# A causal depthwise convolution: five of eight channel tiles as block Toeplitz products

## The chip, the cores and the metric

The kernel runs on one core of one Trainium2 chip. The metric is the device time of one execution in microseconds (us). The core has TensorE (PE, with its weight loads shown apart as PEld), VectorE (DVE), ScalarE (ACT), GpSimd (POOL) and SyncE (SP); each works through its own list of instructions in order. SP issues nearly all DMA transfers.

## The reference

A decoder trunk of two layers on x of 512 positions by 1024 features, in float32:

```
layer 0: mix = [S5 state space | stick-breaking attention](x W_in) W_out
layer 1: h = x W_pw1 + b;  h = h[:, :1024] * sigmoid(h[:, 1024:])
         h[t, c] = sum_k w_dw[k, c] * h[t - 30 + k, c] + b_dw[c]      (31 taps, causal)
         mix = silu(LN(h)) W_pw2 + b
each layer:  x = LN(alpha x + mix);  x = LN(alpha x + relu(x W1 + b1)^2 W2 + b2)
```

The hidden width of the feed-forward layers is 4096. The change bears on layer 1's depthwise convolution.

## The kernel before, in words

Features lie on the partitions: x is eight tiles of 128 features by 512 positions. Every matrix product is made in three products of float32r operands, each operand split into a rounded high part and a low part (`whi`, `wlo`, `xbh`, `xbl`): high by high, high by low, low by high. The class `Weights` loads a weight chunk with SP (`raw`, two buffers), rounds it on ACT (`whi`, L90) and subtracts on DVE (`wlo`, L91), a few units ahead of the product that uses them, into a ring of 3 + 5 slots. Tiles in the trace bear the names of the code: `f` and `acf` are the two products of a feed-forward block, `hh` and `hl` its hidden activations' parts, `pl` the first pointwise product (pw1) of the convolution's tiles 0 and 1, `pv` and `pg` value and gate of the others, `tld` the second pointwise product (pw2), `fl` the next feed-forward layer's first.

The program's stages by the trace: the mix layer to 246 us, its output product and LN a to 306, feed-forward layer 0 to 598 (four blocks of eight hidden tiles), its tail and LN b to 651, pl to 673, the convolution to 812, the second half of LN c and pw2 (tld) to 871, then LN d, feed-forward layer 1 and the transposed output.

The convolution before: a tile's gated input (`hp`, with 30 columns of zeros ahead) is convolved by PE and DVE together. PE takes the first taps of a tile, each as three products with a diagonal 128x128 matrix of the tap's weights, which ACT has made just before (`dh`, `dl`, L136); how many is a table, PE_TAPS. DVE takes the others as multiply-and-add over the whole tile into two accumulators (`cy`, `cz`, L339). The last two tiles are worked in halves of 256 columns, so that the first half of the norm (LN c: `mpc`, `vpc`, `sc`, `sqc`) and of pw2 can begin before their second halves are convolved:

```python
PE_TAPS = ((5, 8, 10, 10, 9, 11, 17, 16), (10, 10, 10, 10, 10, 10, 13, 14))
SPLIT_TILES = 2
```

The order of the work comes from the order in which the code is written and from a scheduler, which places instructions of each engine by their priority and by modelled times; in the mix layer a list of words (`ORDER`) sets it. Thirteen small loads of bias and norm vectors (`rows`) and two transposes of them (`pvp`, L606) stand ahead of that list's steps.

Of the kernel before, what the change touches and what calls it, by code (L numbers as in the profile page):

```python
# [16 lines left out]
P = 128  # L17
# [18 lines left out]
PE_TAPS = ((5, 8, 10, 10, 9, 11, 17, 16), (10, 10, 10, 10, 10, 10, 13, 14))  # L36
DBUFS = 6
SPLIT_TILES = 2
GLU_FIRST = True
FFN_BLOCKS = ((8, 8, 8, 8), (8, 8, 6, 4, 6))  # L40
LEAD = 6
AHEAD = (5, 4)
# [7 lines left out]
ORDER = "q0 s0 y0 s1 y1 a0 q1 s2 y2 a1 s3 y3 q2 gelu a2 q3 glu a3".split()  # L50


class Weights:


    def __init__(self, tc, ahead):
        self.tc, self.nc, self.ahead = tc, tc.nc, ahead
        self.slots, self.units, self.raw, self.urgent, self.fence, self.hold = [], [], None, True, None, False
        self.done, self.got, self.chunk, self.ready = 0, 0, {}, {}
# [17 lines left out]
    def _prep(self, n):  # L77
        nc = self.nc
        while self.done < min(n, len(self.units)):
            key, src, nk, ncol, off, width = self.units[self.done]  # L80
            self.fetch(self.done)
            raw = self.chunk[key][:, :, off : off + ncol]
            pool, s = self.slots[self.done % len(self.slots)]
# [43 lines left out]
class Act:  # L127
# [5 lines left out]
    def __call__(self, out, in_, func, **kw):  # L133
# [10 lines left out]
        self.run.append(ins.name)  # L144


@with_exitstack
def kernel(ctx: ExitStack, tc: tile.TileContext, a: dict, out: bass.AP):
# [442 lines left out]


    rows = s5.tile([P, 2, P], F32, tag="sp", name="rows", bufs=6)
    G.memset(rows, 0.0)
    for n in vecs:
        src = a[n].rearrange("a (r f) -> (a r) f", f=P)
        r0, m = vrow[n], a[n].shape[0] * a[n].shape[1] // P
        done = 0
        while done < m:
            half, at = divmod(r0 + done, P)  # L600
            c = min(m - done, P - at)
            nc.sync.dma_start(rows[at : at + c, half, :], src[done : done + c])
            done += c
    pvp = zz("pvp")
    for i in range(2):
        PE.transpose(pvp[:, i * P : (i + 1) * P], rows[:, i, :], ident)  # L606
    V.tensor_copy(PV, pvp[:, :nrow])
# [132 lines left out]
    for o in ORDER:  # L740
        if o[0] == "q":
            hq[o[1]] = qkv(int(o[1]))
        elif o[0] == "a":
            attention(int(o[1]), *hq[o[1]])
        elif o[0] == "s":
            s5_states(int(o[1]))
        elif o[0] == "y":
            s5_outputs(int(o[1]))
        elif o[0] == "t":
            tables(int(o[1]))  # L750
        elif o == "gelu":
            gelu()
        else:
            glu()

    def accum(nps, xk, name, ncol, first=True, cols=((0, T),)):
# [3 lines left out]
        for c0, c1 in cols:  # L760
            for j in range(KT):
# [7 lines left out]
                else:  # L769
                    tt(x, x, ps[:, c0:c1], ALU.add)  # L770

# [25 lines left out]

    units = units_of("mo", w_out, 4, 4, range(0, D, 256), 512)
    for layer in range(2):
        if layer:  # L800
            for j in range(0, D, 128):
                units += units_of("pw1", a["conv_w_pw1"][0], 0, 8, [j], 256)
                units += units_of("pw1", a["conv_w_pw1"][0], 0, 8, [D + j], 256)
# [15 lines left out]
    class LN:  # L819


        def __init__(self, name):
            self.n, self.s = name, {}

        def add(self, j, ys, c0, c1):

            if j == 1:
                self.s[c0] = tmp(f"s{self.n}{c0}")[:, c0:c1]
            if j:
                (V if j == KT - 1 else G).tensor_tensor(self.s[c0], ys[0][:, c0:c1] if j == 1 else self.s[c0], ys[j][:, c0:c1], op=ALU.add)  # L830
# [53 lines left out]
    class Tail:  # L884
# [7 lines left out]
        def run(self, n):  # L892

            nj = KT // len(self.xk)
            for _ in range(n):
# [9 lines left out]
                self.ln.add(j, X, c0, c1)  # L905
# [39 lines left out]
    def ffn1(layer, bi, k0, nb, xs, fps, first=()):  # L945
        hs = []
        for i in range(nb):
# [12 lines left out]
            hs.append((hh, hl))  # L960
        return hs
# [7 lines left out]
    xs, first = tail_norm_lead(cat[4:8], "a", rb[0], ("ln1_g", 0), ("ln1_b", 0), LEAD, "fl0")  # L969
    k0 = 0  # L970
    for bi, nb in enumerate(FFN_BLOCKS[0]):
        hs = ffn1(0, bi, k0, nb, xs, nps, first if bi == 0 else ())
        if bi < len(FFN_BLOCKS[0]) - 1:
            accum(nps, hs, f"f0{bi}", 1024 // nb, bi == 0)
        k0 += nb
    wdw = hid.tile([P, KT, CONV], F32, tag="wdw", name="wdw")
    for f in range(2):
        wn = tmp(f"wn{f}")[:CONV]
        nc.sync.dma_start(wn, a["conv_w_dw"][0][:, f * T : (f + 1) * T])
        ps = stp(f"wd{f}")  # L980
        for i in range(4):
            PE.transpose(ps[:, i * 32 : i * 32 + CONV], wn[:, i * P : (i + 1) * P], ident[:CONV, :CONV])
        V.tensor_copy(wdw[:, 4 * f : 4 * f + 4, :], ps[:, :P].rearrange("p (i t) -> p i t", t=32)[:, :, :CONV])
    wdh = hid.tile([P, KT, CONV], F32R, tag="wdh", name="wdh")
    wdl = hid.tile([P, KT, CONV], F32, tag="wdl", name="wdl")
    V.tensor_copy(wdh, wdw)
    V.tensor_sub(wdl, wdw, wdh.bitcast(F32))

# [3 lines left out]
    acc = [None] * KT  # L992
    hps = [None] * KT
    cps = [None] * KT

    def glu_tile(j, c0=0, c1=T):
        if c0 == 0:
            if j < 2:
                ps[j] = first[2 * j : 2 * j + 2]
            else:  # L1000
                ws[j], ps[j] = (W.next(), W.next()), (nps(f"pv{j}"), nps(f"pg{j}"))
            hps[j] = hpage(f"hp{j}", F32, PAD + T), hpage(f"hph{j}", F32R, PAD + T), hpage(f"hpl{j}", F32R, PAD + T)
        vps, gps = ps[j]
        if j >= 2:
            gemm(vps, ws[j][0], slice(0, P), xs, c0, c1)
            gemm(gps, ws[j][1], slice(0, P), xs, c0, c1)
        sg = tmp(f"csg{j}{c0}")
        act(sg[:, c0:c1], gps[:, c0:c1], AF.Sigmoid, bias=pv("conv_b_pw1", 8 + j))
        hp, hh, hl = hps[j]
        p0 = PAD + c0 if c0 else 0  # L1010
        if c0 == 0:
            V.memset(hp[:, :PAD], 0.0)
        stt(hp[:, PAD + c0 : PAD + c1], vps[:, c0:c1], pv("conv_b_pw1", j), sg[:, c0:c1], ALU.add, ALU.mult)
        split(hh[:, p0 : PAD + c1], hl[:, p0 : PAD + c1], hp[:, p0 : PAD + c1])

    def taps_pe(j, c0=0, c1=T):
        _, hh, hl = hps[j]
        if c0 == 0:
            cps[j] = nps(f"cv{j}")
        n = PE_TAPS[c0 > 0][j]  # L1020
        for t in range(n):
            dh = hid.tile([P, P], F32R, tag="dh", name=f"dh{j}{t}", bufs=DBUFS)
            dl = hid.tile([P, P], F32R, tag="dl", name=f"dl{j}{t}", bufs=DBUFS)
            act(dh, ident, AF.Copy, scale=wdh.bitcast(F32)[:, j, t : t + 1])
            act(dl, ident, AF.Copy, scale=wdl[:, j, t : t + 1])
            for i, (u, v) in enumerate(((dh, hh), (dh, hl), (dl, hh))):
                PE.matmul(cps[j][:, c0:c1], u, v[:, t + c0 : t + c1], start=t == 0 and i == 0, stop=t == n - 1 and i == 2)  # L1027

    def taps_dve(j, c0=0, c1=T):

        hp = hps[j][0]
        if c0 == 0:
            acc[j] = page(f"cy{j}", F32), hpage(f"cz{j}", F32)
        y, z = (x[:, c0:c1] for x in acc[j])
        t = CONV - 1
        act(y, hp[:, t + c0 : t + c1], AF.Identity, bias=pv("conv_b_dw", j), scale=wdw[:, j, t : t + 1])
        t = CONV - 2
        opened = act(z, hp[:, t + c0 : t + c1], AF.Copy, scale=wdw[:, j, t : t + 1])
# [159 lines left out]
```

## Time and profile before

| what | value |
|---|---|
| median of 3 runs | 1244.07 us (1242.49 to 1245.63) |
| the profiled execution | 1245.87 us, its span 1244.2 us |
| TensorE clock granted, mean | 0.984 |
| PE busy | 1198.7 us, 96% of the span |
| DVE / ACT / POOL busy | 778.6 / 567.7 / 105.8 us |
| DMA moved | 105.93 MB, mean 85 GB/s |

In the profile, rows are groups of instructions or links of the chain that ended last; a row names start, duration, engine, tiles and line, or for groups the busy time, the mean duration of one in ns and the idle time ahead of them with its releaser.

### The profile page before, as it was taken

How to read it: one execution, taken by the hardware profiler on the slowest of the kernel's cores; microseconds unless marked ns; L12 is line 12 of the kernel's file. 1: busy time of each engine (PE TensorE's matmuls, PEld its weight loads, DVE VectorE, ACT ScalarE, POOL GpSimd, SP SyncE). 2: the span in 40 equal slices, each digit the busy share in tenths (PEclk: the TensorE clock that was granted, in tenths of full speed). 3: DMA queues.
4: the chain of work that ended last, by engine and by line, in shares of the span. 5: the costliest groups of instructions: out<-in, count | busy, mean ns of one | idle time of the engine just before them, and what ended most of it. 6: DMA issues, size and time to landing. Idle time of an engine off the chain costs nothing.

```text
span 1244.2 us, 16659 instructions
## 1 busy us (share of the span) xinstructions
PE 1198.7 (96%) x6559; PEld 1016.9 (82%) x6559; DVE 778.6 (63%) x1321; ACT 567.7 (46%) x1020; POOL 105.8 (9%) x145
## 2 busy tenths in 40 slices
PE   9899999999999999999999999689899999999997
PEld 7677776789988888888999889689898888888885
DVE  7897784568734434434388999999863443444446
ACT  6735665734523313314246666876472232323230
POOL 1001100122000000000130012113400000000000
PEclk9999998999999999999999999889899999999999
DMA  8510131050522333322232121003052232323211
GB/s 207 161 36 18 35 110 60 21 200 1 186 88 100 102 102 102 100 81 91 73 103 86 51 68 35 1 28 110 17 186 68 85 119 68 124 68 113 86 51 68
DMA packets 111663, 105.93 MB, mean 85 GB/s; under 512 B 9379, under 2 KB 99747, under 8 KB 111585
## 3 DMA queue, kind: packets, MB, share of 16 engines
q1 hardware_dynamic: 111424, 104.84, 26.9%
q8 instruction: 51, 0.84, 0.3%
q14 instruction: 28, 0.22, 0.1%
q10 hardware_dynamic: 160, 0.03, 0.0%
HBM read 100.66 MB, written 4.19 MB: 84 GB/s over the span
## 4 chain that ended last, share of the span: by engine, by line
PE 75%; DVE 15%; ACT 5%; DMA 2%; issue 2%; POOL 1%; SPq 0%; DVEq 0%; ACTq 0%; POOLq 0%
PE f L207 23%; PE g L1128 11%; PE acf L207 11%; PE fl L207 4%; PE h L1112 3%; PE tld L207 3%; DVE cz L339 3%; PE tlb L207 2%; PE cv L1027 2%; DVE wlo L91 2%; DVE cy L339 2%; PE pl L207 1%; PE pv L207 1%; PE pg L207 1%; DVE X L339 1%
## 5 line engine op out<-in xcount | busy, mean ns | idle before, releaser
L90 ACT CAST whi<-raw 128x1024 fp32r<-128x1024 f32 x176 | 183.9, 1049 | 400.1 <-PE f L207 111.9
L91 DVE TENSOR_TENSOR wlo<-raw,whi 128x1024 fp32r<-128x1024 f32 x176 | 219.5, 1251 | 221.0 <-ACT whi L90 220.7
L1128 PE MATMUL g<-whi,hh 128*128 128x512 f32 x208 | 81.5, 392 | 0.0
L1128 PE MATMUL g<-wlo,hh 128*128 128x512 f32 x208 | 81.5, 392 | 0.0
L1128 PE MATMUL g<-whi,hl 128*128 128x512 f32 x208 | 81.4, 391 | 0.0
L207 PE MATMUL f<-xdh,whi 128*128 128x512 f32 x208 | 80.9, 389 | 0.0
L207 PE MATMUL f<-xah,whi 128*128 128x512 f32 x208 | 80.9, 389 | 0.0
L207 PE MATMUL f<-xal,whi 128*128 128x512 f32 x208 | 80.9, 389 | 0.0
L207 PE MATMUL f<-xdh,wlo 128*128 128x512 f32 x208 | 80.9, 389 | 0.0
L207 PE MATMUL f<-xdl,whi 128*128 128x512 f32 x208 | 80.9, 389 | 0.0
L207 PE MATMUL f<-xah,wlo 128*128 128x512 f32 x208 | 80.9, 389 | 0.0
L207 PE MATMUL acf<-hl,whi 128*128 128x512 f32 x192 | 75.2, 392 | 0.0
L207 PE MATMUL acf<-hh,whi 128*128 128x512 f32 x192 | 74.9, 390 | 0.0
L207 PE MATMUL acf<-hh,wlo 128*128 128x512 f32 x192 | 74.7, 389 | 0.0
L197 ACT CAST hh<-fr 128x512 fp32r<-128x512 f32 x64 | 39.7, 621 | 71.4 <-DVE fr L335 71.4
L198 DVE TENSOR_TENSOR hl<-fr,hh 128x512 fp32r<-128x512 f32 x64 | 44.2, 691 | 37.3 <-ACT hh L197 37.2
L339 DVE SCALAR_TENSOR_TENSOR cy<-hp,wdw,cy 128x512 f32<-128x512 f32 (+1 forms) x91 | 60.8, 678 | 0.1
L339 DVE SCALAR_TENSOR_TENSOR cz<-hp,wdw,cz 128x512 f32<-128x512 f32 (+1 forms) x86 | 59.7, 698 | 0.0
L1027 PE MATMUL cv<-hph,dh 128*128 128x256 f32 (+1 forms) x113 | 40.0, 354 | 10.0 <-ACT hph L197 8.3
L335 DVE TENSOR_TENSOR fr<-fr 128x512 f32<-128x512 f32 x64 | 43.7, 685 | 5.4 <-ACT fr L136 5.4
L1128 PEld LDWEIGHTS g<-whi,hl 128*128 128x128 f32 x208 | 39.1, 188 | 8.6
L1128 PEld LDWEIGHTS g<-wlo,hh 128*128 128x128 f32 x208 | 39.1, 188 | 8.5
(684 smaller groups left out, 3172.3 us busy)
## 6 DMA issues: line engine op xcount, KB each, us to landing
raw<-in_ffn_w_dram SPq DMA_DIRECT2D x48, 1024.0 KB, 5.3
raw<-in_ffn_w_dram SPq DMA_DIRECT2D x32, 512.0 KB, 3.6
raw<-in_conv_w_pw_dram SPq DMA_DIRECT2D x12, 1024.0 KB, 5.4
raw<-in_mix_w_in_dram SPq DMA_DIRECT2D x16, 512.0 KB, 4.2
xin<-in_x_dram SPq DMA_DIRECT2D x8, 256.0 KB, 3.8
raw<-in_s_w_glu_dram SPq DMA_DIRECT2D x4, 512.0 KB
raw<-in_mix_w_out_dram SPq DMA_DIRECT2D x4, 512.0 KB
raw<-in_mix_w_out_dram SPq DMA_DIRECT2D x2, 1024.0 KB, 6.3
```

Source lines behind the costliest of these rows:

```text
L90: i0 = nc.scalar.copy(hi, raw).ins
L91: i1 = nc.vector.tensor_sub(lo, raw, hi.bitcast(F32)).ins
L197: i0 = S.copy(hi, src).ins
L198: i1 = V.tensor_sub(lo, src, hi.bitcast(F32)).ins
L207: ins = PE.matmul(ps[:, c0:c1], u[:, k, ksl], v[:, c0:c1], start=start and k == 0 and i == 0, stop=stop and k == n - 1 and i == 2).ins
L335: V.tensor_tensor(o, x, y, op=op)
L339: V.scalar_tensor_tensor(o, x, s, y, op0=op0, op1=op1)
L1027: PE.matmul(cps[j][:, c0:c1], u, v[:, t + c0 : t + c1], start=t == 0 and i == 0, stop=t == n - 1 and i == 2)
L1112: PE.matmul(ps, u, v, start=k == 0 and i == 0, stop=k == nk - 1 and i == 2)
L1128: PE.matmul(pss[b], u, v[:, kk, :], start=k + kk == 0 and i == 0, stop=k + kk == nb - 1 and i == 2)
```

## The change

1. Tiles 2 to 6 are convolved wholly on PE. A tile's input is laid out in four time phases: 32 channels by four phases make the 128 partitions, so that a product with a 128x128 matrix of Toeplitz blocks takes four taps at once for four phases of output. Nine shifts cover the 31 taps; with four groups of 32 channels and three products each, a tile takes 108 products of 128 columns.
2. The matrices are made on DVE in feed-forward layer 0 from block 1 on: 90 multiplications of 128x512 (`m`), each a broadcast of tap weights times a mask, one pair behind a hidden tile or an accumulation (`make`). SP writes each (256 KB) to DRAM (`made`). The tap weights come by way of DRAM too (`Wd`, `w4`: 16 small loads for each tile).
3. In the convolution POOL reads the matrices back with 50 transfers, two for a unit of eight matrices (512 KB each, high and low parts), through a second `Weights` (`M`) that has four slots of the ring; units of pw1 use the other four.
4. The input's phase layout is made by a round trip through DRAM (`Hd`, four loads `hr`); the output of tiles 6, 2 and 3 goes back the same way (`Od`, `cq`), that of tiles 4 and 5 by sixteen 32x128 operations, half on ACT and half on DVE.
5. Tiles 0, 1 and 7 are convolved wholly on DVE: 29 multiply-and-adds each. There are no halves any more. The work's order is a list of words (`CONV_ORDER`).
6. LN c takes a provisional centre from the first five finished tiles, subtracts it and adds up squares as tiles come; the rest of the mean follows with the last tile. Its sums are on DVE instead of POOL.
7. The `rows` loads and pvp's transposes move into the mix layer's list, behind `a0`.

```diff
-PE_TAPS = ((5, 8, 10, 10, 9, 11, 17, 16), (10, 10, 10, 10, 10, 10, 13, 14))
-DBUFS = 6
-SPLIT_TILES = 2
+ON_PE = (2, 3, 4, 5, 6)
+CONV_ORDER = "g0 g1 d0 g6 d0 d0 d1 g7 d0 s6 g2 d1 m6 o6 d1 x1 f6 d1 s2 g3 m2 o2 d7 x0 s3 d7 g4 m3 f2 o3 d7 d7 s4 g5 c0 m4 s5 f3 e4 m5 e5".split()
-ORDER = "q0 s0 y0 s1 y1 a0 q1 s2 y2 a1 s3 y3 q2 gelu a2 q3 glu a3".split()
+ORDER = "q0 s0 y0 s1 y1 a0 rows q1 s2 y2 a1 s3 y3 q2 gelu a2 q3 glu a3".split()
...
+            if key[0] == "made":
+                w = tuple(pool.tile([P, nk, ncol], F32R, tag=f"w{x}{s}", name=f"w{x}{self.done}", bufs=1) for x in ("hi", "lo"))
+                for x, d in zip(w, src):
+                    nc.gpsimd.dma_start(x.rearrange("p k n -> p (k n)")[:, : d.shape[1]], d)
...
+    bias4 = hid.tile([P, KT, 4], F32, tag="bias4", name="bias4")
+    for q in range(4):
+        nc.sync.dma_start(bias4[32 * q : 32 * q + 32], a["conv_b_dw"][0].rearrange("(j g c) -> c j g", g=4, c=32))
+
+    def matrices(i):
...
+        for p_ in range(4):
+            for g in range(4):
+                nc.sync.dma_start(wr[32 * p_ : 32 * p_ + 32, NU * g : NU * (g + 1)], Wd[32 * g : 32 * g + 32, i, p_ : p_ + NU])
+        V.tensor_copy(wh, wr)
+        V.tensor_sub(wl, wr, wh.bitcast(F32))
+        for u in range(0, 4 * NU, 16):
+            for x, src in enumerate((wh.bitcast(F32), wl)):
+                m = tmp(f"m{j}{x}{u}", F32R)
+                V.tensor_tensor(m.rearrange("p (u c) -> p u c", c=GROUP), src[:, u : u + 16].unsqueeze(2).broadcast_to([P, 16, GROUP]),
+                                mask.unsqueeze(1).broadcast_to([P, 16, GROUP]), op=ALU.mult)
+                nc.sync.dma_start(made[j][x][:, u * GROUP : (u + 16) * GROUP], m.bitcast(F32))
+            yield
...
-            accum(nps, hs, f"f0{bi}", 1024 // nb, bi == 0)
+            accum(nps, hs, f"f0{bi}", 1024 // nb, bi == 0, after=make if bi else None)
...
+    def toeplitz(j):
+
+        hh, hl = hps[j]
+        cp = nps(f"cv{j}")
+        for g in range(4):
+            o = cp[:, g * P : (g + 1) * P]
+            for e in range(SHIFTS):
+                n = SHIFTS * g + e
+                if n % 8 == 0:
+                    w = M.next()
+                mh, ml = (x[:, n % 8] for x in w)
+                for k, (u, v) in enumerate(((mh, hh), (mh, hl), (ml, hh))):
+                    PE.matmul(o, u, v[:, g, e : e + P], start=e == 0 and k == 0, stop=e == SHIFTS - 1 and k == 2)
...
+        elif o[0] == "m":
+            toeplitz(j)
+        elif o[0] == "c":
+            center()
...
-        for j in range(n, KT):
-            taps_dve(j, c0, c1)
...
+        r = conv_norm(c0, c1)
```

In `CONV_ORDER` g makes a tile's gated input, s splits its phases, m makes its products, o, f and e bring it back, d is a piece of eight taps on DVE, c the provisional centre, x prepares the residual.

Three places in the engines' lists. First DVE within feed-forward layer 0, where `fr` and `hl` make a hidden tile and `wlo` a weight's low half. Before:

```order
L335 TENSOR_TENSOR fr_3909<-fr_3909 128x512
L198 TENSOR_TENSOR hl_3913<-fr_3909,hh_3912 128x512
L91 TENSOR_TENSOR wlo_4030<-raw_4027,whi_4029 128x1024
L335 TENSOR_TENSOR fr_3945<-fr_3945 128x512
L198 TENSOR_TENSOR hl_3949<-fr_3945,hh_3948 128x512
```

and after:

```order
L1045 TENSOR_TENSOR m_4085<-w4h_3850,mask 128x512
L1045 TENSOR_TENSOR m_4088<-w_3849,mask 128x512
L351 TENSOR_TENSOR fr_4078<-fr_4078 128x512
L106 TENSOR_TENSOR wlo_4178<-raw_4134,whi_4177 128x1024
L214 TENSOR_TENSOR hl_4082<-fr_4078,hh_4081 128x512
L1045 TENSOR_TENSOR m_4127<-w4h_3850,mask 128x512
```

Two multiplications have come in with each hidden tile, and stand ahead of the next one's `fr`.

Second PE at the end of the convolution. Before, the last products of a first half, with the first mean product between them, and pw1 of other halves ahead:

```order
L207 MATMUL pg_6904<-xbh_5443,wlo_6565 128x256
L1027 MATMUL cv_6988<-hph_6731,dh_7457 128x256
L1027 MATMUL cv_6988<-hpl_6732,dh_7457 128x256
L1027 MATMUL cv_6988<-hph_6731,dl_7458 128x256
L838 MATMUL mpc_7366<-sc_6393,ones 128x256
L1027 MATMUL cv_6988<-hph_6731,dh_7464 128x256
```

and after:

```order
L1117 MATMUL cv_7585<-hl_7547,whi_7614 128x128
L1117 MATMUL cv_7585<-hh_7546,wlo_7615 128x128
L1204 MATMUL mpc_7729<-cy_7550,ones 128x256
L1204 MATMUL mpc_7729<-cy_7559,ones 128x256
L1205 MATMUL vpc_7730<-sqc_7398,ones 128x256
L1204 MATMUL mpc_7729<-cy_7702,ones 128x256
L1206 MATMUL vpc_7730<-sqc_7723,ones 128x256
```

All convolution products now stand ahead of the norm's, and nothing of the convolution stands between them any more; `cy_7702` is the last tile's output.

Third SP in the same stage, after the change (before, it has only raw weights there):

```order
L71 DMA raw_7865<-in_conv_w_pw_dram 128x8x256
L1093 DMA Hd_7150<-hp_7145 128x544
L1097 DMA hr_7152<-Hd_7150 32x4x136 x4
L1125 DMA Od_7294<-cr_7292 128x512
L1129 DMA cq_7296<-Od_7294 32x4x128 x4
L1093 DMA Hd_7387<-hp_7382 128x544
L1097 DMA hr_7389<-Hd_7387 32x4x136 x4
L71 DMA raw_7875<-in_conv_w_pw_dram 128x8x256
```

The round trips of tiles 4 and 5 stand with the output of tile 3 between two loads of pw2's weights.

More of the change, by code (lines that the diff above doesn't have):

```diff
@@ L960, in ffn1 @@
             hs.append((hh, hl))
+            if layer == 0 and bi:
+                make()
         return hs
@@ L970, with make @@
+    def make():
+        for _ in range(1):
+            next(making, None)
+    making = (None for i in range(NT) for _ in matrices(i))
     k0 = 0
     for bi, nb in enumerate(FFN_BLOCKS[0]):
+        if bi == 1:
+            taps()
         hs = ffn1(0, bi, k0, nb, xs, nps, first if bi == 0 else ())
         if bi < len(FFN_BLOCKS[0]) - 1:
-            accum(nps, hs, f"f0{bi}", 1024 // nb, bi == 0)
+            accum(nps, hs, f"f0{bi}", 1024 // nb, bi == 0, after=make if bi else None)
         k0 += nb
-    wdw = hid.tile([P, KT, CONV], F32, tag="wdw", name="wdw")
@@ L977 @@
[L977 to L985, printed above, removed]
@@ L1016, in taps_pe @@
[L1016 to L1027, printed above, removed]
```

332 lines of the change are left out of this document (233 added, 99 removed).

## The prediction

> **What bounds the kernel now.** I read the page's busy times first, then the busy times stage by stage, then the chain that ended last.
>
> ```profile
> span 1244.2 us, 16659 instructions
> PE 1198.7 (96%) x6559; PEld 1016.9 (82%) x6559; DVE 778.6 (63%) x1321; ACT 567.7 (46%) x1020; POOL 105.8 (9%) x145
> ```
>
> The profiled execution took 1245.87 us, 1.8 above the median of the runs (1244.07); its span is 1244.2. All sums below are differences against the profile, laid on the median. PE is idle for 45 us of the span, so only where it idles, or is made to do less, can anything be won. By stage (columns: length, PE, PEld, DVE, ACT, POOL busy, granted clock, DMA share, GB/s):
>
> ```profile
> 306.00:598.00 292.00, 291.87 (x1358) 244.03 (x1358) 130.25 (x154) 99.60 (x125) 0.00 (x0) 1.00 0.33 105
> 673.00:728.00 55.00, 55.00 (x243) 45.06 (x242) 54.70 (x82) 38.31 (x88) 0.89 (x1) 1.00 0.25 79
> 728.00:812.00 84.00, 73.14 (x459) 66.17 (x457) 83.33 (x151) 61.08 (x174) 14.89 (x14) 0.93 0.08 26
> 812.00:871.00 59.00, 56.19 (x431) 55.07 (x432) 55.09 (x118) 40.95 (x90) 18.00 (x19) 0.95 0.23 72
> ```
>
> The first feed-forward layer (306 to 598) is PE's: DVE has 162 us to spare there and the DMA engines two thirds. The convolution (673 to 812) has PE full until 728; from there DVE is full (83.33 of 84) and PE waits 10.9 us, 8.3 of them in one gap. The chain, in order, at the places that count:
>
> ```profile
> 661.40 12.00 PE pl L207 x96
> 673.41 3.66 PE cv L1027 x15
> 677.07 5.44 PE pv L207 x24
> 682.51 5.45 PE pg L207 x24
> 704.43 6.94 PE cv L1027 x30
> 769.46 2.67 DVE cz L339 x4
> 799.42 0.85 PE mpc L838 x2
> 807.76 1.28 ACT L138
> 812.26 7.77 PE tld L207 x43
> 859.44 11.51 PE tld L207 x96
> 870.94 2.88 PE fl L207 x24
> ```
>
> And of the view of waits the one of PE on a convolution product (us in total, times, longest):
>
> ```profile
> PE cv L1027 <- ACT hph L197: 8.3, 1, 8.3
> ```
>
> So DVE's taps (cy, cz) set the time from 728 to 798; then the norm's first half, the pointwise product (tld) from 812.26, and the next layer (fl) from 870.94. I compare 812.26 and 870.94 with the changed kernel.
>
> **The convolution's products and taps.** Before, PE makes 53 taps of 512 columns and 60 of 256, three products each. A 512-column one takes 6.94/30 = 0.231 us, a 256-column one 11.51/96 = 0.120: 36.8 + 21.6 = 58.4 us. After, it makes 5 tiles x 4 groups x 9 shifts x 3 = 540 products of 128 columns. The trace has no such float32r run; nearest are eight 128x128 transposes and a run of weight loads whose starts lie 0.11 apart:
>
> ```profile
> 59.03 0.87 PE gp L502 x8
> ...
> 101.91 0.19 PEld L677 LDWEIGHTS z0C<-sl0B,negs 128*128 128x128 f32 x1
> 102.02 0.19 PEld L677 LDWEIGHTS z0C<-sh0C,tri 128*128 128x128 f32 x1
> 102.12 0.19 PEld L677 LDWEIGHTS z0C<-sl0C,tri 128*128 128x128 f32 x1
> ```
>
> 0.87/8 = 0.109 us each, 58.9 us in all; the low end is half of a 256-column one (0.060, 32 us), the high end 0.120 (65 us). I take 0.109, because each product needs a fresh 128x128 load and the loads follow at 0.11. PE's work is then unchanged: nothing is won on PE. The Trainium skill, "TensorE: Matmul & The Clock Gate", section "Back-to-back issue gap", states a sustained 81 ns for N=128 in streams of load and product; by it the 540 would take 43.7 us, 15 less. The rows above speak for 0.11.
>
> DVE's taps fall from 177 to 87 (three tiles of 29):
>
> ```profile
> L339 DVE SCALAR_TENSOR_TENSOR cy<-hp,wdw,cy 128x512 f32<-128x512 f32 (+1 forms) x91 | 60.8, 678 | 0.1
> L136 ACT ACTIVATE dh<-ident,wdh 128x128 fp32r<-128x128 f32 x107 | 41.9, 392 | 1.1 <-PE cv L1027 1.1
> L335 DVE TENSOR_TENSOR fr<-fr 128x512 f32<-128x512 f32 x64 | 43.7, 685 | 5.4 <-ACT fr L136 5.4
> L91 DVE TENSOR_TENSOR wlo<-raw,whi 128x1024 fp32r<-128x1024 f32 x22 | 28.9, 1318 | 2.1 <-ACT whi L90 2.0
> ```
>
> Some 60 us leave DVE and the 2 x 107 diagonals (84 us) leave ACT, so PE becomes the bound. Walking PE's order: pl ends at 673.4; six tiles of pv and pg at 5.44 + 5.45 make 65.4; the 540 products 58.9; the centre's product 0.9: the last Toeplitz product ends at 798.6 if no operand is late.
>
> **What now stands behind it.** Before, the norm's first half hid behind other tiles' taps; now all columns of tile 5 come last, and PE waits for it.
>
> ```profile
> 800.35 2.73 DVE L335 TENSOR_TENSOR cy<-cy,mpc 128x256 f32<-128x256 f32 x8
> L142 ACT ACTIVATE cy<-cy,PV 128x256 f32<-128x256 f32 x16 | 9.2, 597 | 2.6 <-DVE cy L335 2.6
> ```
>
> The first row is the eight subtractions of one half now, the second the silu of a 128x256 piece. By these and the rows above: copy out of PSUM 0.7 (fr's width), eight 32x128 pieces on ACT 2.4 (0.39 each as dh, less their overlap), minus the centre 0.7 and square 0.4, mean and variance products 0.9 (two at mpc's 0.43), the root's steps 3.0 (four of about 0.4 and a table load of 1.28), 2.7 of subtractions of which the root hides about half, then product, silu, cast and low part of the first piece 0.3 + 0.6 + 0.4 + 0.4. That is 11 to 13, taken as 12 us, so tld starts at 810.6: 1.7 earlier than 812.26. The 10.9 us that PE waits for taps are thus mostly paid again for the norm. From tld to fl: 384 products at 0.120 are 46.1, the next norm's 1.8. The low half of the fourth pw2 unit stands on DVE behind the second half's norm and I charge 4.5 us for it; the gap ahead costs clock, as it does now:
>
> ```profile
> 793.70:803.90 10.20, 5.85 (x23) 5.38 (x24) 9.63 (x27) 6.54 (x20) 1.56 (x3) 0.50 0.00 1
> 810.80:817.60 6.80, 6.17 (x28) 5.88 (x29) 6.77 (x21) 6.80 (x19) 0.26 (x1) 0.50 0.01 2
> ```
>
> Half a clock over 6.8 us, partly waiting anyway: 2.2. Together 54.6 against 58.7 now: -4.1. Term: -1.7 - 4.1 = -5.8.
>
> **Reading the matrices back.** POOL issues 50 transfers, two of 512 KB a unit, into four slots. No transfer of POOL's is in the trace; the nearest are SP's:
>
> ```profile
> raw<-in_ffn_w_dram SPq DMA_DIRECT2D x48, 1024.0 KB, 5.3
> raw<-in_ffn_w_dram SPq DMA_DIRECT2D x32, 512.0 KB, 3.6
> U<-Ud SPq DMA_DIRECT2D x16, 64.0 KB, 3.8
> out_dram<-X SPq DMA_DIRECT2D x8, 256.0 KB, 2.2
> ```
>
> 512 KB more takes 1.7 us more, so a stream of 1 MB units goes at 3.4 us a unit. PE eats a unit (24 products) in 2.6, a tile's 4.5 in 11.8. With pv and pg between them a tile has 22.7 us for 4.5 units (15.3): enough. Tiles 4 and 5 follow without a pause: with four units in, the fifth to tenth come into freed slots, and the ninth is needed at 19.6 and there at about 20.4: about 1 us late. At 5.3 a unit the last is 5.5 late. The activations make a round trip (out 2.2, four pieces back 3.8, issues 1.7: about 8); tile 5's has some 2 us to spare at m5 and shares the engines with these units. I take +2, ends 0 and +5.5.
>
> **Making them.** 90 broadcast multiplications of 128x512 on DVE, at 0.685 (the fr row), 62 us, over three blocks (218 us), where DVE's share now is 130.25 x 218/292 = 97: 159 of 218, so the spare time covers them. But they stand between the accumulations that free PSUM and the low halves PE needs, with 90 writes and 80 small gathers (0.4 us of SP each) ahead of raw weights: +0.5, ends 0 and +6. The writes, 23.6 MB, double the 105 GB/s; the DMA share goes to about 0.66. If the cover goes, PE waits for a low half (hl).
>
> **The rows.** Thirteen vector loads and pvp's transposes move from ahead of the mix layer's first steps to behind a0:
>
> ```profile
> 58.73 0.30 PE L606 MATMUL pvp<-ident,rows 128*128 128x128 f32 x1 [3.02 <-DMA rows<-in_conv_b_pw_dram]
> ```
>
> ```profile
> DVE Gx L335 <- PE tp L510: 5.7, 3, 4.5
> ```
>
> PE's 3.0 us wait goes, and SP's other loads come earlier; but DVE waits 4.5 for tp right behind, and the order after it shifts. I take -2.5: the 3.0 less a little for what is late next (Gx); ends -4.5 (the loads' early landing on top) and +1.5.
>
> **Small transfers.** Four loads of bias4 (4096 packets of four bytes) stand on SP ahead of mix_w_out's last loads.
>
> ```profile
> DMA packets 5421, 0.67 MB, mean 134 GB/s; under 512 B 5356, under 2 KB 5419, under 8 KB 5419
> ```
>
> ```profile
> 252.21 1.05 ACT L90 CAST whi<-raw 128x1024 fp32r<-128x1024 f32 x1 [4.71 <-DMA raw<-in_mix_w_out_dram]
> 260.53 1.05 ACT whi L90
> ```
>
> The first row is 5 us (15 to 20) with 5421 mostly small packets, the engines nearly full, so 4096 take under 4 us. The cast that waits for these loads comes at 252.21; the chain enters ACT only at 260.53, with a cast that waits for a buffer of PE's. Between them lie 8 us, so nothing; high end +3, if the next raw loads, which wait for these casts, move along. The early centre adds a handful of DVE steps within PE's cover.
>
> **Sum.** -5.8 + 2 + 0.5 - 2.5 = -5.8: 1238 us. A difference under 0.3% (3.7 us) can't be told from no change here.
>
> **Rivals.** (a) Slower: the read-back bounds the stage. At 3.4 us a unit it doesn't; a tile's 22.7 us are exceeded from 22.7/4.5 = 5.0 a unit on, and at about 5.3 the sum is near zero. At 5.6, three tiles lose 2.5 each and the last pair about 8: +15.7 - 2 in place of the +2, 1252. Against it: SP's difference of 1.7 a half; for it: no row shows POOL's queue, and two transfers done one after the other are 7.2 by the 3.6 row. By the Trainium skill, "DMA: Bandwidth & Descriptors", section "Anatomy of one DMA — SWDGE (gpsimd) path", 2.0 us + bytes/436 GB/s, an estimated 3.2 us for each 512 KB; without overlap that would be 6.4 a unit and beyond this rival, with overlap as I take it. No run shows which. 0.2.
> (b) 128-column products go well under 0.109: at 0.081, a unit lasts 1.9 us and the read-back takes part of it back: about 1226 to 1230. 0.07.
> (c) No difference: the norm behind the last tile, the clock and the wait for the pw2 unit eat it, or the multiplications stall the feed-forward layer by 3 to 6 us: 1241 to 1247. 0.18.
>
> **Numbers.** My forecast 0.55 (1232 to 1240); with (b) and small parts, faster 0.62, same 0.18, slower 0.20. The range is 1226 (b, or both gains without stall) to 1253 (a).
>
> **What would show it.** Right: cv x540 on PE at 0.11 a start; PE full from 673 to about 800, then one idle stretch of about 12 us; DVE below 80% there; 306 to 598 unchanged within 1 us; pvp without a wait. Wrong: cv waits on DMA of whi (rival a) or of hr; hl or acf waits in the blocks; weights arriving late at 252 to 270.

## The result, and the profile after

The changed kernel takes 1261.59 us (median of 4 executions, 1257.10 to 1261.81), the kernel before beside it 1243.76 (1242.49 to 1245.63): ratio 1.0131, interval 1.0111 to 1.0151. It is 1.3% slower; I had forecast 1238 and a range to 1253. The profiled execution took 1261.79 us.

The first two lines of the page after: PE is now 15 us busier, DVE 13 us busier (the multiplications, less the taps that PE took over), ACT 65 us less.

```profile
span 1260.1 us, 17113 instructions
PE 1213.6 (96%) x6674; PEld 1033.4 (82%) x6674; DVE 791.8 (63%) x1347; ACT 502.9 (40%) x801; POOL 113.0 (9%) x177
```

Where the difference of 15.9 us between the two spans lies, by the starts of instructions on PE (us; "no trip" is an experiment told below, which leaves the inputs' round trips through DRAM out):

| stage | before | after | no trip | predicted change | change |
|---|---|---|---|---|---|
| start to the first f of layer 0 (rows) | 325.7 | 320.0 | 319.1 | -2.5 | -5.7 |
| f to the end of pl (making matrices) | 347.6 | 348.3 | 348.3 | +0.5 | +0.7 |
| end of pl to the first tld (convolution) | 139.0 | 159.6 | 139.7 | -1.7 + 2 | **+20.6** |
| first tld to the first fl (pw2) | 58.5 | 56.3 | 56.4 | -4.1 | -2.2 |
| fl to the end | 373.4 | 375.9 | 376.1 | 0 | +2.5 |

One stage holds it. Its stretches in the table of busy times (columns: length, PE, PEld, DVE, ACT, POOL busy with counts, granted clock, DMA share, GB/s) are, from the top, tile 6's Toeplitz products, tile 3's, those of tiles 4 and 5, and the norm behind them:

```profile
700.60:712.60 12.00, 12.00 (x110) 11.96 (x108) 12.00 (x18) 1.74 (x2) 4.11 (x8) 1.00 0.83 237
752.50:776.00 23.50, 23.15 (x107) 22.96 (x108) 14.03 (x19) 4.38 (x9) 4.22 (x8) 0.50 0.64 204
789.90:814.30 24.40, 24.40 (x218) 24.15 (x216) 13.64 (x25) 11.83 (x23) 6.32 (x12) 1.00 0.75 239
814.40:827.80 13.40, 7.74 (x22) 5.02 (x21) 9.78 (x30) 8.41 (x19) 0.00 (x0) 0.75 0.00 1
```

The same 108 products take 12.0 us in tile 6 and 23.6 in tile 3, at a granted clock of 0.50 for the whole of it. The chain of work that ended last shows what stands ahead of tile 3:

```profile
731.50 1.06 DVE hp L355
732.58 15.80 DMA Hd<-hp
749.76 2.04 DMA hr<-Hd
753.33 23.09 PE cv L1117 x107
776.41 7.78 PE pv L223 x24
790.50 24.08 PE cv L1117 x216
827.87 9.18 PE tld L223 x60
```

A store of 272 KB (`Hd`, tile 3's input on its way to DRAM) takes 15.8 us. PE's last gate product (pg) starts at 746.35 and tile 3's first at 752.57: 6.2 us, of which some 6.0 are waiting (products of pg otherwise start 0.23 apart). Its waits name ACT's rounding of the input just read back:

```profile
PE cv L1117 <- ACT hh L1101: 5.8, 1, 5.8
```

The pause ends at half clock, and tile 3 stays there: its 108 products take 23.6 us instead of 12.0, 11.6 more. The full clock comes back only in the 512-column products behind it (the next pv takes 7.78 for 24, 2.3 too long). So 6.0 + 11.6 + 2.3 = 19.9 of the stage's 20.6 us; the other 0.7 is there without the trips too. The clock carries more than twice what the wait itself carries.

Why the store took so long is seen on SP's queue and in the DMA view of 736 to 740 us (columns: packets, MB, share of 16 engines):

```profile
724.40 7.53 SPq L71 DMA_DIRECT2D raw<-in_conv_w_pw_dram  x2
732.58 0.34 SPq L1093 DMA_DIRECT2D Hd<-hp  x1
748.44 1.75 SPq L1097 DMA_DIRECT2D hr<-Hd  x4
```

```profile
DMA packets 652, 1.47 MB, mean 369 GB/s; under 512 B 32, under 2 KB 358, under 8 KB 652
...
q0 software_dynamic: 286, 1.07, 74.2%
q1 hardware_dynamic: 366, 0.41, 35.3%
```

Two 1 MB loads of pw2's weights stand ahead of it in the same queue, and beside that queue (q1) POOL's reading back of matrices (q0) takes most of the engines. A packet of q0 is 3.7 KB on the mean (1.07 MB / 286), one of q1 1.1 KB (0.41 / 366); the two move packets at a like pace, so q0 gets 72% of the bytes. The Trainium skill, "DMA: Bandwidth & Descriptors", section "Queues, rings and completion order", says that each engine goes round between its queues packet by packet; the rows agree in kind, though not one for one.

DVE itself was late with tile 3's `hp`, by some 5 us (with that step moved, in the second repair below, the store is issued at 727.30 instead of 732.58): ACT's sigmoid for that tile stood behind the activation of a tile-6 piece that waited 6.86 us for the way back from DRAM (`cq`).

```profile
726.07 1.40 ACT L151 ACTIVATE cy<-cq,PV 128x128 f32<-128x128 f32 x4 [6.86 <-DMA cq<-Od]
728.90 0.68 ACT L157 ACTIVATE csg<-pg,PV 128x512 f32<-128x512 f32 x1
```

### The profile page after: what moved, and what is told of

Its sections match the earlier page's. It is cut to its first block, busy times and chain, and to the rows that moved or that the text cites. A ratio compares the mean times of both kernels' runs of the same rounds, so it can differ in the third digit from the quotient of the medians.

```text
span 1260.1 us, 17113 instructions
## 1 busy us (share of the span) xinstructions
PE 1213.6 (96%) x6674; PEld 1033.4 (82%) x6674; DVE 791.8 (63%) x1347; ACT 502.9 (40%) x801; POOL 113.0 (9%) x177
## 5 line engine op out<-in xcount | busy, mean ns | idle before, releaser
L106 DVE TENSOR_TENSOR wlo<-raw,whi 128x1024 fp32r<-128x1024 f32 x176 | 218.1, 1244 | 180.7 <-ACT whi L105 180.2
L1117 PE MATMUL cv<-hh,whi 128*128 128x128 f32 x180 | 54.8, 305 | 5.8 <-ACT hh L1101 5.8
L214 DVE TENSOR_TENSOR hl<-fr,hh 128x512 fp32r<-128x512 f32 x64 | 44.0, 689 | 23.7 <-ACT hh L213 23.6
L1117 PE MATMUL cv<-hl,whi 128*128 128x128 f32 x180 | 54.5, 303 | 0.3 <-DVE hl L1102 0.3
L1117 PE MATMUL cv<-hh,wlo 128*128 128x128 f32 x180 | 54.5, 303 | 0.0
L1309 PEld LDWEIGHTS g<-whi,hh 128*128 128x128 f32 x208 | 39.0, 188 | 8.8
```

Of the source, the lines that this page charges most:

```text
L106: i1 = nc.vector.tensor_sub(lo, raw, hi.bitcast(F32)).ins
L214: i1 = V.tensor_sub(lo, src, hi.bitcast(F32)).ins
L1117: PE.matmul(o, u, v[:, g, e : e + P], start=e == 0 and k == 0, stop=e == SHIFTS - 1 and k == 2)
L1309: PE.matmul(pss[b], u, v[:, kk, :], start=k + kk == 0 and i == 0, stop=k + kk == nb - 1 and i == 2)
```

## The experiments

Theory: the round trip of tile 3's input is late behind weight loads, and the pause it makes takes PE's clock, which a stream of 128-column products cannot win back. Rivals: the reading back of the matrices is the bound; the 128-column stream is slow by itself; the new norm or the made matrices cost it.

### Filling the pause: 27 and 34 wide products, and 20 in the middle

Dummy products of 512 columns stand ahead of tile 3's, 27 in the first kernel and 34 in the second:

```diff
+        if j in FILL:                           # FILL = {3: 27}, then {3: 34}
+            dum = stp(f"dum{j}")
+            with tc.issue_after(last["pe"]):
+                for i in range(FILL[j]):
+                    behind = PE.matmul(dum, xs[0][0][:, :P], xs[0][0], start=True, stop=True).ins
...
+                    if behind is not None:
+                        tc.add_manual_dep(ins, behind.name, NOSYNC, reason="behind the filler")
...
```

Expected of 27:

> The changed kernel with 27 idle 512-column products (results unused) on PE between tile 4's gate and tile 3's Toeplitz products, where PE sat idle for 6.2 us. Theory 1 (the pause costs the clock, and a stream of 128-column products doesn't win it back): the wait for hr3 stays, so those 6.2 us stay, but the 108 products of tile 3 run at 0.11 us instead of 0.219 and tile 5's gate product at 0.23: 14 us less, about 1247 us. Rival (tile 3's products are slow for another reason, units read back late or the engines' ports): 0.219 stays, about 1262 us.

Measured: 1258.26 us (1255.78 to 1274.14; the one execution of 1274.14 is not explained), ratio 1.0142 (1.0075 to 1.0210). The 27 ended at 750.96, a little too early: PE paused 0.16 us ahead of tile 3's first product and 0.65 ahead of the second, and 3.4 us later the clock was gone:

```profile
751.00:754.50 3.50, 3.07 (x26) 2.81 (x25) 3.37 (x6) 3.03 (x5) 0.00 (x0) 1.00 0.20 75
754.50:772.40 17.90, 17.90 (x86) 17.90 (x86) 10.67 (x14) 1.40 (x4) 4.21 (x8) 0.50 0.82 246
```

So less than 1 us of waiting in a 128-column stream was enough here (a like wait in a later run, below, was not). Expected of 34:

> As the run with 27 idle products, with 34 (7.7 us), which reach past the arrival of tile 3's low half at about 752.3, so that PE doesn't pause at all ahead of tile 3's products. With 27 it still paused for 0.16 and then 0.65 us, and the clock fell 3.4 us later. Theory 1 (a pause of under 1 us in a stream of 128-column products is enough to lose the clock, none leaves it): tile 3's 108 products at 0.111, cv of tile 3 to 5 without half clock, about 1247 us. Rival (something in tile 3 itself, its units or its operands): 0.2 us a product again, 1257 us.

Measured: 1275.04 us, ratio 1.0251 (1.0236 to 1.0266). Tile 3 now ran at full clock, in half the time; but all behind it moved, tile 4's input (its store issued at 764.29, its read back only at 777.76) made PE pause 5.2 us, and the 216 products of tiles 4 and 5 took the half clock:

```profile
753.30:765.30 12.00, 12.00 (x109) 11.96 (x109) 11.65 (x15) 2.24 (x6) 4.09 (x8) 1.00 0.69 203
782.00:828.50 46.50, 46.22 (x216) 46.03 (x216) 15.54 (x28) 13.21 (x25) 6.33 (x12) 0.50 0.46 137
```

The time that I expected was missed, by tiles of which I had not thought; both rows say the same of the clock. With 20 wide products put behind the first 27 of tile 3's own 108, the pause is left and only the recovery is tried:

```diff
+            if (j, g) in WIDE:                  # WIDE = {(3, 0): 20}
+                dum = stp(f"dum{j}")
+                with tc.issue_after(ins):
+                    for i in range(WIDE[j, g]):
+                        behind = PE.matmul(dum, xs[0][0][:, :P], xs[0][0], start=True, stop=True).ins
```

> The changed kernel with 20 idle 512-column products on PE after the first 27 of tile 3's 108, the pause ahead of them left as it is. Theory 1 (a stream of 128 columns can't win the clock back, a few us of 512 columns can): tile 3's first 27 products at 0.219, the wide ones at 0.43 and after one or two windows 0.23, then the last 81 at 0.111; about 4 us less than the changed kernel, 1257 us. Rival (the half clock lasts a fixed 25 to 30 us once it has come): all 108 at 0.219 and 20 x 0.43 = 8.6 us more, 1270 us.

Measured: 1252.63 us (one execution), some 9 less than the changed kernel although PE does more. By the traces 6.7 of it are in this stage, 1.3 of them a shorter pause (4.9 instead of 6.2); 2.6 stand ahead of the first f, where the two kernels are the same. In the table of busy times, the 27, the wide ones, the other 81:

```profile
748.70:755.00 6.30, 6.00 (x27) 5.81 (x28) 6.12 (x10) 3.28 (x6) 0.27 (x1) 0.50 0.26 83
755.00:761.20 6.20, 6.20 (x23) 4.97 (x23) 6.06 (x8) 1.06 (x4) 0.79 (x2) 0.74 0.32 86
761.20:770.10 8.90, 8.90 (x82) 8.90 (x80) 1.84 (x3) 0.00 (x0) 3.03 (x6) 1.00 0.98 334
```

Six microseconds of 512-column products (755.08 to 761.19) bring the clock back, and the 128-column ones then keep it, with the matrices read back beside them at a DMA share of 0.98. The stream is not slow by itself.

### The clock alone

A kernel of nothing but PE streams, with pauses between (its output is a copy of x):

```diff
+PLAN = [(0, [(512, 80), (128, 300)]), (20, [(128, 300), (512, 60)]), (20, [(256, 150)]), (20, [(384, 100)]),
+        (20, [(512, 80)]), (10, [(128, 200), (512, 60)]), (5, [(128, 200), (512, 60)]), (2, [(128, 200), (512, 60)])]
```

Each entry is a pause (in ACT steps) and then streams of (columns, products), every product with a fresh 128x128 load.

> Only streams of PE products (float32r, a new 128x128 load for each) with pauses of some 13, 7, 5 and 3 us between them, in place of the whole computation; the output is a copy of x. Theory 1: after a pause of 13 us a stream of 128 columns stays at half clock (0.219 us a product) for its whole length, a stream of 512 columns is at full clock after some 3 to 7 us; a 128-column stream that follows a warm 512-column one stays at 0.11. Rival (the clock comes back after some us whatever the width): 0.11 after the first 3 to 10 us of the 128-column stream too. 256 and 384 columns show where between them it turns.

```profile
21.00:56.00 35.00, 35.00 (x304) 34.53 (x303) 0.00 (x0) 0.00 (x0) 0.00 (x0) 1.00 0.01 1
71.00:137.00 66.00, 65.57 (x304) 65.28 (x305) 0.00 (x0) 0.89 (x2) 0.00 (x0) 0.50 0.00 0
137.00:150.00 13.00, 13.00 (x57) 10.70 (x56) 0.00 (x0) 0.00 (x0) 0.00 (x0) 0.96 0.01 1
165.00:185.00 20.00, 19.76 (x150) 19.55 (x150) 0.00 (x0) 0.46 (x2) 0.00 (x0) 0.91 0.00 1
389.00:425.00 36.00, 36.00 (x171) 36.00 (x170) 0.00 (x0) 0.00 (x0) 0.00 (x0) 0.50 0.00 0
```

First row: 128-column products (from 23.6 on) behind 512-column ones, full clock, 0.112 us each. Second: 300 of them behind a pause of 14.5 us, half clock and 0.214 us each for all of their 64 us, although PE never waits (65.57 of the row's 66 us busy). Third: the 512-column products that follow begin at 135.5, and the row's 0.96 puts the return of the full clock at 138.0, 2.5 us later (3.2 to 5.3 us in the three entries that follow). Fourth: 256-column products win it back by themselves, 0.91 over their 20 us; 384 and 512 columns do so too (0.90 and 0.89). Last: a pause of 2.7 us was enough for 128-column products to lose the clock and stay at half until wide ones came. So the effect needs no DMA, no other engine and no particular kernel.

The Trainium skill, "TensorE: Matmul & The Clock Gate", section "HAM oscillation — how this bites in real kernels", puts it as "no PE-idle gaps >~3.4µs", and section "What's actually happening" has the clock full after about 3.4 us of sustained work. The changed kernel's own pause of 6 us fits the first; otherwise both differ here: pauses of 2.7 us, and once of 0.16 + 0.65 us in a narrow stream, sufficed, and 64 us of unbroken 128-column products did not bring it back. The measurement decides; what it is in a stream that keeps or returns the clock was not tried.

### Taking away what the store stands behind

First, pw2's weight loads are held behind the read-back of each round trip:

```diff
...
+            if key[0] == "pw2" and self.behind:
+                self.tc.add_manual_dep(ins, self.behind, NOSYNC, reason="behind the round trips")
...
+            W.behind = nc.sync.dma_start(hps[j][32 * p_ : 32 * p_ + 32], hv[p_]).ins.name
```

> The changed kernel with the loads of pw2's first two weight chunks (1 MB each) moved on SP from ahead of tile 3's round trip to behind tile 3's and behind tile 4's. Theory 1a (Hd3 was late because 2 MB stood ahead of it in its own queue): Hd3 lands in 2 to 5 us instead of 15.8, PE's 6.2 us wait goes and with it the half clock: 20 us less, about 1241 us. Rival 1b (POOL's read-back alone holds it up, since its queue takes the engines): Hd3 still takes over 10 us, the wait and the clock stay, 1255 to 1262 us.

Measured: 1266.93 us, ratio 1.0181 (1.0151 to 1.0211). On SP's queue:

```profile
731.07 0.34 SPq L1096 DMA_DIRECT2D Hd<-hp  x1
734.75 2.68 SPq L1100 DMA_DIRECT2D hr<-Hd  x4
```

The store is 3.7 us now instead of 15.8, so it takes those loads to make it long. But the pause before tile 3 was still 2.9 us: the last of the four pieces came only at 747.8, 13 us after the first was issued, beside POOL's stream and a weight load issued behind them. That was enough for the half clock; within tile 5 PE paused 1.95 and 1.3 us and lost it too:

```profile
748.50:772.00 23.50, 23.07 (x108) 22.93 (x108) 15.72 (x22) 4.42 (x8) 4.23 (x8) 0.51 0.61 176
801.20:823.80 22.60, 22.59 (x106) 22.60 (x107) 1.92 (x3) 1.45 (x4) 1.06 (x2) 0.50 0.38 125
```

Those two waits in tile 5 are not for a trip. They name the matrices, high and low, so in this order of the queue the reading back itself was late:

```profile
PE cv L1120 <- DMA whi<-madeh: 1.7, 1, 1.7
PE cv L1120 <- DMA wlo<-madel: 1.0, 1, 1.0
```

Second, tile 3's trip alone is protected, and the step that held up ACT (f6) goes behind the gate of tile 3. Third, the next pw2 load is held behind tile 4's trip as well:

```diff
-CONV_ORDER = "... x1 f6 d1 s2 g3 m2 o2 ..."
+CONV_ORDER = "... x1 d1 s2 g3 f6 m2 o2 ..."
...
+            if key[0] == "pw2" and i < 114:     # third kernel; in the second all of pw2 behind tile 3
+                self.tc.add_manual_dep(ins, self.behind[3 + (i >= 112)], NOSYNC, reason="behind a round trip")
```

> The changed kernel with two moves, nothing added: tile 6's way back (f6) stands behind tile 3's gate on ACT and DVE, so that tile 3's input is not held up by tile 6's round trip; and pw2's first weights are loaded behind tile 3's round trip. Theory 1: Hd3 starts at about 726 instead of 732.6 and lands in 3 to 5 us, tile 3's operands are there before PE needs them at 746, no pause, no half clock until tile 5's products end: 20 us less, 1239 to 1243 us, that is not distinguishable from before or a little faster, and some 3 us behind the kernel before with the vector loads moved alone. Rival (the read-back stream bounds the last two tiles at full clock, which the half clock hid): pauses in tile 4 or 5, half clock there, 1255 us or more.

Measured: 1268.07 us, ratio 1.0196 (1.0179 to 1.0212). Tile 3 has no pause and runs at 0.111. The weight load that was held back now stands one place ahead of tile 4's store:

```profile
755.00 0.39 SPq L72 DMA_DIRECT2D raw<-in_conv_w_pw_dram  x1
756.04 0.34 SPq L1096 DMA_DIRECT2D Hd<-hp  x1
770.86 1.74 SPq L1100 DMA_DIRECT2D hr<-Hd  x4
775.00:821.60 46.60, 46.30 (x216) 46.12 (x217) 15.57 (x28) 13.28 (x25) 6.33 (x12) 0.50 0.45 136
```

(The last row is of the table of busy times.) Tile 4's store now lasts 14.8 us, PE pauses 4.7, and two tiles lose the clock instead of one. Of the third kernel:

> The run with the two moves, and the third pw2 chunk also moved on SP, from ahead of tile 4's round trip to behind it; in the run with two moves tile 4's write Hd4 stood behind that chunk for 14.8 us, PE paused 4.7 us and tiles 4 and 5 ran at half clock. Theory 1 (each round trip is late where a weight load stands just ahead of it while POOL reads units): Hd4 lands in 4 us, no pause before any tile, no half clock until tile 5's products end, 1268 - 4.7 - 23 - 2 = 1238 us. Rival (the read-back can't feed tiles 4 and 5 at full clock): pauses on whi within tile 4 or 5 and the half clock again, 1250 us or more.

Measured: 1262.90 us, ratio 1.0166 (1.0135 to 1.0197). Tile 4's store is down to 6.8 us and PE pauses only 0.64 us ahead of tile 4's first product and 0.65 us behind it. The clock still goes, 3.4 us later:

```profile
771.00:774.40 3.40, 2.92 (x25) 2.71 (x24) 2.63 (x4) 3.38 (x5) 0.00 (x0) 1.00 0.31 112
774.40:815.50 41.10, 41.10 (x195) 41.10 (x195) 12.95 (x25) 10.01 (x21) 6.35 (x12) 0.50 0.50 148
```

Each repair moved the lateness to a later tile. In none of these three orders of SP's queue were all trips and matrices on time beside pw2's weights. Whether another order of the tiles would make them so was not tried.

### Less to read back

Only one low matrix of each unit of eight is read back, 13 MB instead of 23.6 (the other low products use that one, so the values differ):

```diff
-                for x, d in zip(w, src):
-                    nc.gpsimd.dma_start(x.rearrange("p k n -> p (k n)")[:, : d.shape[1]], d)
+                for i, (x, d) in enumerate(zip(w, src)):
+                    n = 128 if i else d.shape[1]
+                    nc.gpsimd.dma_start(x.rearrange("p k n -> p (k n)")[:, :n], d[:, :n])
...
-                mh, ml = (x[:, n % 8] for x in w)
+                mh, ml = w[0][:, n % 8], w[1][:, 0]
```

> The changed kernel with most of the low matrices' read-back left out (of each unit of eight only the first low matrix is read and stands for all eight): 13 MB instead of 23.6 through POOL's queue, PE's work the same. Theory 1 (Hd3 is late because POOL's 4 KB packets take two thirds of the engines while 2 MB of 1 KB packets stand ahead of it): Hd3 lands in 6 to 9 us instead of 15.8, PE waits less than 1 us or not at all ahead of tile 3, and the time falls to 1241 us if the clock holds. Rival (SP's own queue is slow for another reason, its weight loads alone): Hd3 still takes over 13 us, pause and half clock stay, 1260 us.

Measured: 1256.97 us (one execution). Tile 3's store takes 6.5 us, although the same two weight loads are issued 8.2 us ahead of it as in the changed kernel: POOL's full stream is needed for the 15.8 us as much as the loads are.

```profile
721.20 7.52 SPq L71 DMA_DIRECT2D raw<-in_conv_w_pw_dram  x2
729.37 0.34 SPq L1094 DMA_DIRECT2D Hd<-hp  x1
735.88 1.75 SPq L1098 DMA_DIRECT2D hr<-Hd  x4
```

PE does not pause ahead of tile 3, which has full clock. Tile 5's input is still late by 2.9 us, and tile 5 goes at half clock. Tile 4 shows what the runs before do not: PE paused 0.13 us ahead of its first product (770.40) and 0.65 us ahead of its second, nearly as with the 27 wide products (0.16 and 0.65), and here the clock stayed full:

```profile
770.40:773.80 3.40, 3.13 (x26) 2.83 (x25) 2.73 (x4) 3.25 (x4) 0.00 (x0) 1.00 0.21 77
773.80:782.40 8.60, 8.60 (x80) 8.60 (x78) 6.56 (x11) 3.04 (x5) 3.40 (x7) 1.00 0.92 238
```

A wait of this size can cost the clock and need not; what decides stays open.

### No round trip at all

Tiles' inputs go to the products without `Hd` and `hr` (the values are therefore not the convolution's); everything else stays.

```diff
-        Hd = tc.dram_tile([P, 4, P + 8], F32, name=f"Hd{j}")
-        nc.sync.dma_start(Hd, hp)
-        hps[j] = hpage(f"hr{j}", F32, PAD + T + 2).rearrange("r (g m) -> r g m", g=4)
...
+        hps[j] = hp
```

> The changed kernel with the inputs' round trips through DRAM (Hd, hr) left out: the Toeplitz products take the gated input as it lies, so the convolution's values are not the reference's, while all products, read-back, taps and the outputs' way back stay. Theory 1 (the loss is the late inputs and the clock that they cost; the sum of the prediction holds for the rest): no pause between 673 and 800, all 540 products at 0.111 us, the last at 794 to 796, pw2 from 808 or 809, about 1240 us. Rival (without the pauses the read-back is too slow for tiles 4 and 5 in a row): pauses of 1 us or more on whi or wlo in tile 5, then half clock, 1250 us or more.

Measured: 1240.12 us (10 executions, 1238.21 to 1241.55), ratio 0.9972 (0.9960 to 0.9984).

```profile
745.70:757.70 12.00, 12.00 (x109) 11.96 (x108) 4.60 (x6) 3.49 (x7) 4.08 (x8) 1.00 0.84 259
769.10:793.60 24.50, 24.50 (x218) 24.21 (x217) 13.40 (x25) 11.80 (x23) 6.32 (x12) 1.00 0.67 218
```

All 540 products run at 0.111 to 0.113, and no matrix comes late. This settles three things: the round trip and what it does to the clock are the loss (1261.6 to 1240.1); reading the matrices back does not bound the stage when nothing of the trips stands in its way; and even without the loss the convolution and pw2 together gain only 1.4 us (139.7 + 56.4 against 139.0 + 58.5).

### The rows alone

The kernel before with step 7 of the change only:

```diff
-ORDER = "q0 s0 y0 s1 y1 a0 q1 s2 y2 a1 s3 y3 q2 gelu a2 q3 glu a3".split()
+ORDER = "q0 s0 y0 s1 y1 a0 rows q1 s2 y2 a1 s3 y3 q2 gelu a2 q3 glu a3".split()
```

> The kernel before with one part of the change alone: the 13 vector loads and pvp's transposes moved behind a0 in the mix layer's list. The changed kernel was 5.6 us ahead at the first feed-forward layer. If the move made that: 5 to 6 us less than before, about 1238 us, with gp at 52.4 instead of 58.9. If the lead came from something else in the mix layer: within 1 us of before.

Measured: 1238.12 us (10 executions, 1236.74 to 1240.36), ratio 0.9958 (0.9945 to 0.9970). This is the version that beats both kernels, and it needs none of the Toeplitz products.

### Warming the clock ahead of pw2

To the second and third repairs above, 27 wide products were added in the three pauses of the norm behind the last tile:

```diff
+        if c0 == 0:
+            wide(14, part[-1])
...
+        wide((5, 8)[c0 > 0], end)
```

> As the run with the two moves, and 27 idle 512-column products on PE in the three pauses between the last Toeplitz product and pw2 (14, 5 and 8), to keep the clock. In the changed kernel the clock was at half for 17 us between 818 and 849. Theory 1 (these pauses cost PE's clock in pw2): 3 to 5 us less than without them, about 1236 us. Rival (the norm's and DVE's steps bound there and PE would wait anyway): within 1 us of the run without them.

> As the run with all three moves, with the 27 idle 512-column products in the pauses between the last Toeplitz product and pw2. They brought 1.6 us in the run with two moves, where the clock was low at their start; here the clock is full when they begin. Theory 1: 2 to 4 us less than without them, about 1235 us. Rival (DVE's and ACT's norm steps bound there): no difference to the run without them.

Measured: 1266.51 (ratio 1.0189, 1.0171 to 1.0208) and 1262.06 us (1.0156, 1.0129 to 1.0182), 1.6 and 0.8 under the same kernels without them. The intervals overlap, so no gain is shown (and the products ahead of these pauses ran at half clock, where I had expected a full one for the third repair), though in the third repair's table of busy times the clock behind the norm rises from 0.72 to 1.00 (829 to 835; without them, then with):

```profile
829.00:835.00 6.00, 6.00 (x39) 6.00 (x39) 5.73 (x18) 5.95 (x14) 0.00 (x0) 0.72 0.00 0
```

```profile
829.00:835.00 6.00, 6.00 (x52) 6.00 (x52) 5.76 (x18) 5.95 (x14) 0.00 (x0) 1.00 0.00 0
```

## Why the prediction was wrong, point by point

**The failed step** is the one on reading back: "The activations make a round trip (out 2.2, four pieces back 3.8, issues 1.7: about 8) ... I take +2, ends 0 and +5.5." It failed twice. Its price came from transfers with nothing ahead of them: out 2.2 became 15.8, because two 1 MB weight loads stand just ahead in SP's queue (I had shown the trips of tiles 4 and 5 between such loads, and priced neither), and because POOL's stream, which I had priced only for the matrices, takes most of the engines beside it. And no term or rival priced a late operand at more than its own lateness: 6.0 us of waiting cost 19.9. I had priced the clock only ahead of tld, at 2.2 us, in products of 256 columns. The term measured +19.9 (159.6 us of the stage with the trips, 139.7 without) against a high end of +5.5. A wait of cv on hr was on my list of signs, without this price. I had looked for the danger at tile 5; it came at tile 3, and at tile 4 or 5 in every repair that helped tile 3's trip.

**Rival (a)**, the matrices' own stream as the bound at 1252, did not happen: no product waited for `whi` or `wlo` of a matrix in the changed kernel, nor in the version without trips, at a DMA share of 0.84. Of all the versions it shows in one, 1.7 and 1.0 us in tile 5 with pw2's loads behind the trips. It had the sign of the change, for a reason that isn't there.

**PE's products**: 0.109 predicted, 0.111 to 0.113 measured; rival (b), 0.081, fell. The rows of weight loads and transposes were the right neighbours. 324 at 0.111 and 216 at 0.113 are 60.5 us against 58.9 in the sum.

**The norm behind the last tile**: 12 predicted, 13.6 measured in both versions (814.3 to 827.87; 793.54 to 807.16). With the products' 1.6 this is what turns -1.7 into +0.7 in the version without trips (the two would make it +1.5; 0.8 comes back ahead of them).

**pw2**: the wait for the fourth unit's low half was 4.3 us where I had 4.5:

```profile
822.52 0.58 PE L223 MATMUL tld<-csh,wlo 128*128 128x256 f32 x1 [4.29 <-DVE wlo L106]
```

(Version without trips.) The stage came to 56.4 instead of 54.6, a gain of 2.2 and not 4.1 (by the first starts the stage before is 58.5; I had taken 58.7 from the chain). In that trace the granted clock is 0.88 on the mean over its first 14.6 us and 0.51 over the next 6.9, in which PE is busy for 6.2: some 4.8 us by these figures (an estimate, 0.12 x 14.6 + 0.49 x 6.2) where I had charged 2.2.

**Making the matrices**: +0.5 predicted. Layer 0 itself, f to the next stage's first product, lost 2.0 us (273.0 to 275.0), the tail and LN b behind it gave 1.3 of that back, so +0.7 on the path. The 90 multiplications took 0.686 us each, 62 in all as estimated; DVE's busy time in the layer rose by 46 us and was covered (what makes up the difference was not taken apart); before, then after:

```profile
325.70:598.70 273.00, 273.00 (x1203) 225.25 (x1202) 113.19 (x129) 84.73 (x103) 0.00 (x0) 1.00 0.31 100
```

```profile
320.00:594.90 274.90, 274.90 (x1209) 225.79 (x1209) 159.66 (x225) 84.59 (x103) 0.00 (x0) 1.00 0.54 175
```

**The rows**: -2.5 predicted with ends -4.5 and +1.5, -5.7 measured in the trace and -5.2 in the executions of the rows alone (0.42% of 1244). Too cautious: I had counted PE's 3.0 us wait and taken something off for Gx, while the first gp behind it starts 6.5 us earlier (52.4 instead of 58.9); which loads made up the rest was not taken apart. Single traces scatter here with the clock: in that of the rows alone f starts 8.7 us earlier than before (317.0), with a granted clock of 1.00 from 60 to 200 us where the trace before has 0.95. So the executions' 5.2 is the better figure.

**Not in the sum**: +2.5 from fl to the end, 1.5 of it between fl and f (LN d). It is there with and without the trips, so it is not the trips', and not with the rows alone (373.2), so it is not theirs; its cause stays open.

The version without trips has, by its starts before rounding, -6.6 + 0.8 + 0.7 - 2.2 + 2.8 = -4.5 us in its span, and 0.28% (3.5 us) in its executions: at the edge between my forecast and the third case, that norm and clock eat the gain.

## What to carry to other kernels

Before work is moved onto PE as many narrow products, price a late operand at the wait plus the rest of that stream at half clock (in these runs all waits that come to 1.3 us or more at a 128-column stream cost the clock, and one of two that come to 0.8), and plan either slack ahead of its first product or a stretch of wide products within it (6 us sufficed here). A small transfer's price is that of what stands around it in its queue and of the streams beside it: read the order of the queue, not the row of the same size elsewhere. When a change has several parts, run the cheapest alone: here moving thirteen small loads won more than the whole.

## What the runs showed of the hardware

- A stream of 128-column float32r products kept the full clock (0.111 to 0.113 us a product) but did not win it back: 64 us at 0.214 after a pause of 14.5 us. Streams of 256, 384 and 512 columns recovered by themselves (0.89 to 0.91 on the mean over their 20 us).
- Two pauses that sum to 1.3 us (0.64 + 0.65) at the head of such a stream lost it; of two pairs that sum to 0.8 us one lost it (0.16 + 0.65) and one did not (0.13 + 0.65). The loss came about 3.4 us after.
- Two queues that shared the DMA engines moved packets at a like pace, 286 and 366 in 4 us: those of 3.7 KB made 1.07 MB, those of 1.1 KB 0.41 MB. A 272 KB store took 3.7 us with no load ahead, 6.5 with the matrices' stream halved, 15.8 with both.
